# Products of zeros ahead of a decoder layer's first matrix products, two row tiles on a second load queue, and their norms in written order

## The chip, the core and the metric

The kernel runs on one core of a Trainium2 chip. The metric is device time in microseconds (us), the median of the runs. TensorE (PE) has a clock gate with two levels, 1.2 and 2.4 GHz. The other engines are VectorE (DVE), ScalarE (ACT), GpSimd (POOL) and SyncE (SP); SP issues most of the transfers, POOL the rest.

## What is computed

One step of a decoder layer, for a prompt of 2048 rows with 16 learned meta rows ahead of it, and for 64 sample rows (8 sequences of 8). The width is 1024, the type float32.

```python
hn = rmsnorm(x, g_mix_pre)                  # x * rsqrt(mean(x*x) + eps) * g
q, k, v, xl, gate = split(hn @ w_in)        # 3 * 512 + 2 * 512 columns
attn = stick_breaking_attention(q, k, v)    # the samples also read a paged cache
lru = rglru(conv4(xl)) * gelu(gate)
x = x + rmsnorm(concat(attn, lru) @ w_out, g_mix_post)
x = x + rmsnorm(relu(rmsnorm(x, g_mlp_pre) @ w_up) ** 2 @ w_down, g_mlp_post)
```

## The kernel before

The prompt is worked on in four blocks of 512 rows (`NSB = 4`). The meta rows and the samples ride along with block 0, whose input projection has 16 + 512 + 64 = 592 columns in two chunks, 0 to 272 and 272 to 592. Each float32 product is made of three TensorE products of rounded parts: `whi*ahi` (L181), `whi*alo` (L182), `wlo*ahi` (L183). Weights come in tiles of 128x1024 (`wraw`, two buffers, loaded by SP); ACT rounds one into `whi` (L158), and DVE takes the remainder into `wlo` (L159). `whi` and `wlo` have two buffers each, the products' outputs `D` four, the transposes' outputs `T` three.

What the change touches is the start, `first_norms`. It loads six row tiles: the 16 meta rows, four tiles of 128 prompt rows (x0 to x3), the 64 samples. The first weight tile's load stands behind that of x1. Each tile is squared and summed on ACT (`mean_sq`, L244), gets its `ms` on DVE (L233) and its `rstd` on POOL (L237), and is scaled in place on DVE (L397). `part(ci, k)` then transposes slice k of the three tiles of chunk ci on PE (L403) into one `T`; ACT makes `ahi` of it (L406), DVE `alo` (L407). Two parts are made at once; the other 14 are popped one by one before the products of step k in the first `gemm`: eight steps over chunk 0 (three products of 272 columns each), then eight over chunk 1 (320 columns). The last two steps have no part left to pop.

The order of PE's instructions is the written one, for the whole program: `with tc.manual_schedule(engines={ET.PE})`. The order of ACT, DVE, POOL and SP is chosen by the planner of the tile framework from its own estimates, except in the few stretches that also name them. An engine executes its instructions strictly in the order that it was given. `prep` (L420 to L429) loads and scales the rows of the next block in the buffers `y` that x0 to x3 leave; the planner has put it beside the first `gemm`.

Of the kernel before, what the change touches and what calls it, by code (L numbers as in the profile page):

```python
# [8 lines left out]
F32 = mybir.dt.float32  # L9
F32R = mybir.dt.float32r  # L10
# [3 lines left out]
ALU = mybir.AluOpType  # L14
PSUM = bass.MemoryType.PSUM

P = 128
# [16 lines left out]
ET = mybir.EngineType  # L34
# [45 lines left out]
def program(tc, I, O, NSB, NSC):  # L80
    with tc.manual_schedule(engines={ET.PE}):
        _program(tc, I, O, NSB, NSC)


def _program(tc, I, O, NSB, NSC):

    nc = tc.nc
# [4 lines left out]
    def pool(name, side="left", space=None):  # L92
        kw = {"space": space} if space else {}
        cm = tc.tile_pool(name=name, bufs=1, side=side, reuse_waits="tile", **kw)
        p = cm.__enter__()
        pools[side].append((p, cm))
        return p
# [6 lines left out]
    def T(p, shape, dt, tag, bufs=1):  # L104
        uid[0] += 1
        return p.tile(shape, dt, name=f"{tag}_{uid[0]}", tag=tag, bufs=bufs)
# [3 lines left out]
    wp = pool("wp")  # L110
# [3 lines left out]
    def psD():  # L114
        return T(ps, [P, 512], F32, "D", 4)

    def psT():
        return T(ps, [P, 512], F32, "T", 3)
# [3 lines left out]

    ident = T(const, [P, P], F32, "ident")
    nc.sync.dma_start(ident, I["ident"])


    seq = []
# [18 lines left out]
    def w_load(n):  # L146
        if n < len(seq) and n not in wraw:
            t = T(wp, [P, 1024], F32, "wraw", 2)
            nc.sync.dma_start(t, seq[n].rearrange("p a b -> p (a b)"))
            wraw[n] = t  # L150
# [79 lines left out]
    def rstd_of(parts, rows):  # L230
        ms = T(xp_, [P, 1], F32, "ms", 7)
        if len(parts) == 1:
            nc.vector.tensor_scalar(ms[:rows], parts[0], EPS, None, op0=ALU.add)  # L233
        else:
            nc.vector.scalar_tensor_tensor(ms[:rows], parts[0], EPS, parts[1], op0=ALU.add, op1=ALU.add)
        r = T(xp_, [P, 1], F32, "rstd", 7)
        nc.gpsimd.tensor_tensor(r[:rows], ms[:rows], nhalf[:rows], op=ALU.pow)  # L237
        return r

    def mean_sq(src, rows):  # L240
        junk = T(xp_, [P, DM], BF16, "junk", 1)
        ss = T(xp_, [P, 1], F32, "ss", 20)
        w = src.shape[-1]
        nc.scalar.activation(junk[:rows, 0:w], src, AF.Square, scale=1.0 / 32.0, accum_out=ss[:rows])  # L244
        return ss[:rows]

    def xsrc(s, j):
        return I["x_prompt"][(4 * s + j) * P:(4 * s + j + 1) * P, :]
# [129 lines left out]
    def first_norms(p1, ahi, alo):  # L378

        st = lambda: T(p1, [P, DM], F32, "vst", 2)  # L380
        y = lambda: T(xp_, [P, DM], F32, "y", 4)
        tiles = [(0, NMETA, I["meta_tokens"], st)]
        tiles += [(NMETA + P * j, P, xsrc(0, j), y) for j in range(4)]
        tiles.append((NMETA + SB, NSAMP, I["x_sample"], st))
        gT = T(const, [P, 2, KC], F32, "gT")
        xts = []
        for i, (col, rows, src, new) in enumerate(tiles):
            xt = new()
            nc.sync.dma_start(xt[:rows], src)
            xts.append(xt)  # L390
            if i == 2:
                w_load(0)
            if i == 0:
                nc.sync.dma_start(gT, I["gT"])
        for (col, rows, src, _), xt in zip(tiles, xts):
            r = rstd_of([mean_sq(xt[:rows, :], rows)], rows)
            nc.vector.tensor_scalar(xt[:rows], xt[:rows], r[:rows], None, op0=ALU.mult)  # L397

        def part(ci, k):
            t = psT()  # L400
            c0 = tiles[3 * ci][0]
            for (col, rows, src, _), xt in list(zip(tiles, xts))[3 * ci:3 * ci + 3]:
                nc.tensor.transpose(t[:, col - c0:col - c0 + rows], xt[:rows, k * P:(k + 1) * P], ident[:rows, :rows])  # L403
            n = col + rows - c0
            h = ahi[:, k, c0:c0 + n]
            nc.scalar.activation(h, t[:, 0:n], AF.Identity, scale=gT[:, 0, k:k + 1])  # L406
            nc.vector.scalar_tensor_tensor(alo[:, k, c0:c0 + n], t[:, 0:n], gT[:, 0, k:k + 1], h.bitcast(F32),  # L407
                                           op0=ALU.mult, op1=ALU.subtract)

        todo = [(ci, k) for ci in range(2) for k in range(KC)]  # L410
        for _ in range(2):
            part(*todo.pop(0))

        def step(ci, k):
            if todo:
                part(*todo.pop(0))

        return step, gT
# [692 lines left out]
    ahi = T(pa, [P, KC, W], F32R, "ahi")  # L1111
    alo = T(pa, [P, KC, W], F32R, "alo")
    first, gT = first_norms(p1, ahi, alo)
    K = consts(p1, gT)
    work.side = [("s", ("kv", 0), lambda: sample_attn(K, p1))]
# [178 lines left out]
```

## Time and profile before

| | |
|---|---|
| runs | 2788.22, 2781.06 and 2786.87 us; median 2786.87 |
| the profiled execution | 2790.22 us, span 2788.3 us |
| PE busy | 2688.2 us, 96% of the span |
| DVE, ACT, POOL busy | 65%, 52%, 18% |
| mean granted clock of PE | 0.985 of full speed |

The span is the time from the first to the last instruction of the profile; the 1.9 us around it are start and end. Busy shares say which engine is loaded, not which one sets the end of a stage. The matmuls' ends are modelled, so spacing from start to start is what shows PE's pace.

### The profile page before, as it was taken

How to read it: one execution, taken by the hardware profiler on the slowest of the kernel's cores; microseconds unless marked ns; L12 is line 12 of the kernel's file. 1: busy time of each engine (PE TensorE's matmuls, PEld its weight loads, DVE VectorE, ACT ScalarE, POOL GpSimd, SP SyncE). 2: the span in 40 equal slices, each digit the busy share in tenths (PEclk: the TensorE clock that was granted, in tenths of full speed). 3: DMA queues.
4: the chain of work that ended last, by engine and by line, in shares of the span. 5: the costliest groups of instructions: out<-in, count | busy, mean ns of one | idle time of the engine just before them, and what ended most of it. 6: DMA issues, size and time to landing. Idle time of an engine off the chain costs nothing.

```text
span 2788.3 us, 36998 instructions
## 1 busy us (share of the span) xinstructions
PE 2688.2 (96%) x13804; PEld 2219.4 (80%) x13804; DVE 1814.3 (65%) x2790; ACT 1451.6 (52%) x2426; POOL 515.5 (18%) x711
## 2 busy tenths in 40 slices
PE   8999988998899999999999999999999999999998
PEld 6886766777688888887788888878888887998996
DVE  5456364686777777788867777798686436433434
ACT  6556364575665655565555555665555234332332
POOL 5336361341211101112110001120000002000002
PEclk9999998999999999999999999999999999999999
DMA  4465855467534433345443333454333334322223
GB/s 161 134 208 189 261 152 171 134 169 221 166 92 128 119 115 106 106 138 154 154 110 115 103 111 103 138 162 143 105 96 104 112 119 144 99 84 77 83 84 113
DMA packets 177316, 368.23 MB, mean 132 GB/s; under 512 B 49153, under 2 KB 79361, under 8 KB 177137
## 3 DMA queue, kind: packets, MB, share of 16 engines
q1 hardware_dynamic: 103792, 287.35, 32.2%
q0 software_dynamic: 73344, 78.52, 11.3%
q8 instruction: 109, 1.79, 0.3%
q14 instruction: 71, 0.57, 0.1%
HBM read 305.51 MB, written 60.04 MB: 131 GB/s over the span
## 4 chain that ended last, share of the span: by engine, by line
PE 80%; DVE 7%; DMA 5%; POOL 3%; issue 3%; ACT 2%; SPq 0%; POOLq 0%; DVEq 0%; ACTq 0%
PE D L181 11%; PE D L183 11%; PE D L182 11%; PE D L213 10%; PE D L214 10%; PE D L215 10%; PE T L712 4%; PE T L702 4%; PE O L734 2%; PE O L736 2%; DVE wlo L159 1%; DMA md<-pb 1%; DVE pb L648 1%; POOL rstd L237 1%; DMA q<-qd 1%
## 5 line engine op out<-in xcount | busy, mean ns | idle before, releaser
L159 DVE TENSOR_TENSOR wlo<-wraw,whi 128x1024 fp32r<-128x1024 f32 x368 | 464.2, 1261 | 496.1 <-ACT whi L158 495.8
L181 PE MATMUL D<-ahi,whi 128*128 128x512 f32 (+3 forms) x1920 | 709.2, 369 | 0.0
L183 PE MATMUL D<-ahi,wlo 128*128 128x512 f32 (+3 forms) x1920 | 686.3, 357 | 2.0 <-DVE wlo L159 2.0
L182 PE MATMUL D<-alo,whi 128*128 128x512 f32 (+3 forms) x1920 | 685.0, 357 | 2.8 <-DVE alo L1017 1.5
L158 ACT CAST whi<-wraw 128x1024 fp32r<-128x1024 f32 x368 | 386.6, 1050 | 485.5 <-PE D L214 282.8
L213 PE MATMUL D<-whi,uh 128*128 128x512 f32 x1024 | 418.1, 408 | 0.0
L183 PEld LDWEIGHTS D<-ahi,wlo 128*128 128x128 f32 x1920 | 364.8, 190 | 53.2 <-DVE wlo L159 2.9
L181 PEld LDWEIGHTS D<-ahi,whi 128*128 128x128 f32 x1920 | 365.2, 190 | 51.9 <-issue 8.7
L214 PE MATMUL D<-whi,ul 128*128 128x512 f32 x1024 | 405.2, 396 | 0.0
L215 PE MATMUL D<-wlo,uh 128*128 128x512 f32 x1024 | 404.3, 395 | 0.0
L182 PEld LDWEIGHTS D<-alo,whi 128*128 128x128 f32 x1920 | 365.7, 190 | 45.5 <-DVE alo L1017 1.7
L640 ACT ACTIVATE keep<-T,nbias 128x512 f32<-128x512 f32 (+6 forms) x352 | 209.7, 596 | 241.7 <-PE T L702 234.6
L648 DVE TENSOR_TENSOR_SCAN pb<-keep,carry 128x513 f32<-128x513 f32 (+1 forms) x228 | 270.3, 1186 | 71.9 <-ACT keep L640 69.9
L724 DVE TENSOR_TENSOR wtl<-T,wth 128x512 fp32r<-128x512 f32 (+1 forms) x320 | 191.0, 603 | 73.7 <-ACT wth L723 72.6
L723 ACT CAST wth<-T 128x512 fp32r<-128x512 f32 (+1 forms) x320 | 166.1, 523 | 127.6 <-PE T L712 122.7
L215 PEld LDWEIGHTS D<-wlo,uh 128*128 128x128 f32 x1024 | 192.7, 188 | 46.7
L213 PEld LDWEIGHTS D<-whi,uh 128*128 128x128 f32 x1024 | 192.9, 188 | 39.9 <-DVE uf L1032 0.4
L214 PEld LDWEIGHTS D<-whi,ul 128*128 128x128 f32 x1024 | 193.3, 189 | 38.6
L652 DVE TENSOR_TENSOR beta<-beta,pb 128x512 f32<-128x512 f32 (+7 forms) x360 | 208.2, 578 | 0.0
L641 ACT ACTIVATE beta<-T,bias 128x512 f32<-128x512 f32 (+6 forms) x352 | 208.2, 591 | 0.0
L712 PE MATMUL T<-ident,beta 128*128 128x128 f32 (+1 forms) x1216 | 193.7, 277 | 14.1 <-ACT beta L641 7.6
L702 PE MATMUL T<-kv,q 128*128 128x512 f32 (+5 forms) x640 | 180.4, 364 | 10.3 <-ACT beta L641 4.4
(235 smaller groups left out, 3600.0 us busy)
## 6 DMA issues: line engine op xcount, KB each, us to landing
wraw<-in_w_up SPq DMA_DIRECT2D x128, 512.0 KB, 3.5
wraw<-in_w_down SPq DMA_DIRECT2D x128, 512.0 KB, 3.5
wraw<-in_w_in SPq DMA_DIRECT2D x64, 512.0 KB, 3.9
q<-qd POOLq DMA_DIRECT2D x32, 512.0 KB, 16.9
wraw<-in_w_out SPq DMA_DIRECT2D x32, 512.0 KB, 3.5
kv<-kd POOLq DMA_DIRECT2D x48, 256.0 KB, 4.1
kv<-vd POOLq DMA_DIRECT2D x48, 256.0 KB, 4.2
y<-in_x_prompt SPq DMA_DIRECT2D x16, 512.0 KB, 5.6
```

The source lines that it names most:

```text
L158: nc.scalar.copy(hi, r)
L159: nc.vector.tensor_tensor(lo, r, hi.bitcast(F32), op=ALU.subtract)
L181: nc.tensor.matmul(o, whi[:, k, :], ahi(k, a, b), start=(k == 0), stop=False)
L182: nc.tensor.matmul(o, whi[:, k, :], alo(k, a, b), start=False, stop=False)
L183: nc.tensor.matmul(o, wlo[:, k, :], ahi(k, a, b), start=False, stop=(k == KC - 1))
L213: nc.tensor.matmul(o, h, whi[:, kk, :], start=st, stop=False)
L214: nc.tensor.matmul(o, l, whi[:, kk, :], start=False, stop=False)
L215: nc.tensor.matmul(o, h, wlo[:, kk, :], start=False, stop=sp)
L640: nc.scalar.activation(keep[:, o:512], S, AF.Sigmoid, bias=nbias, scale=-0.125)
L648: nc.vector.tensor_tensor_scan(pb[:, o:513][:, ::-1], kr, kr, 1.0 if carry is None else carry, op0=ALU.mult, op1=ALU.bypass)
L702: nc.tensor.matmul(o, H["q"][:, e, i * P:(i + 1) * P], kap, start=(e == 0), stop=(e == 1))
L712: nc.tensor.transpose(t[0:kn, i * P:(i + 1) * P], w[:, c0:c0 + kn], ident)
```

## The change

A tile of zeros is made at the start, in one of the two buffers of `wlo`, by a memset of 640 columns on DVE. TensorE multiplies 128 of its columns with 512 others, 13 times, before anything else; two more such products stand between the first transposes of the meta tile and of x0, and six between those of x0 and x1. Their output, one of the four `D` buffers, is never read. The loads of x0 and x1 go through ScalarE's queue instead of SP's. The norms of the meta tile, x0 and x1 are issued in the written order on DVE, ACT and POOL, that is, tile by tile.

```diff
+    idle = T(wp, [P, 1024], F32R, "wlo", 2)
+    nc.vector.memset(idle.bitcast(F32)[:, 0:640], 0.0)
+    idle_out = psD()
+
+    def idling(n):
+        for _ in range(n):
+            nc.tensor.matmul(idle_out, idle[:, 512:640], idle[:, 0:512], start=True, stop=True)
+
+    idling(13)
...
             xt = new()
-            nc.sync.dma_start(xt[:rows], src)
+
+            (nc.scalar if i in (1, 2) else nc.sync).dma_start(xt[:rows], src)
             xts.append(xt)
...
-        for (col, rows, src, _), xt in zip(tiles, xts):
+        with tc.manual_schedule(engines={ET.DVE, ET.Activation, ET.Pool}):
+            for (col, rows, src, _), xt in list(zip(tiles, xts))[:3]:
+                r = rstd_of([mean_sq(xt[:rows, :], rows)], rows)
+                nc.vector.tensor_scalar(xt[:rows], xt[:rows], r[:rows], None, op0=ALU.mult)
+        for (col, rows, src, _), xt in list(zip(tiles, xts))[3:]:
             r = rstd_of([mean_sq(xt[:rows, :], rows)], rows)
             nc.vector.tensor_scalar(xt[:rows], xt[:rows], r[:rows], None, op0=ALU.mult)
...
-            for (col, rows, src, _), xt in list(zip(tiles, xts))[3 * ci:3 * ci + 3]:
+            for i, ((col, rows, src, _), xt) in enumerate(list(zip(tiles, xts))[3 * ci:3 * ci + 3]):
+                if (ci, k) == (0, 0):
+                    idling((0, 2, 6)[i])
                 nc.tensor.transpose(t[:, col - c0:col - c0 + rows], xt[:rows, k * P:(k + 1) * P], ident[:rows, :rows])
```

## Rows read from the trace of the kernel before

**Rows 1.** The page, part 1: busy us (share of span) xinstructions.

```profile
PE 2688.2 (96%) x13804; PEld 2219.4 (80%) x13804; DVE 1814.3 (65%) x2790; ACT 1451.6 (52%) x2426; POOL 515.5 (18%) x711
```

**Rows 2.** The chain that ended last, 0 to 36 us: start us, us, what.

```profile
2.59 4.58 DMA y<-in_x_prompt
7.25 1.16 ACT junk L244 x2
8.67 1.69 POOL rstd L237
10.38 0.76 DVE y L397
11.19 2.14 PE T L403 x7
```

**Rows 3.** Timeline of PE, 12 to 36 us: start us, us, engine, line, op.

```profile
12.98 0.57 PE L181 MATMUL D<-ahi,whi 128*128 128x272 f32 x1
...
14.49 0.57 PE L181 MATMUL D<-ahi,whi 128*128 128x272 f32 x1
...
27.88 0.47 PE L182 MATMUL D<-alo,whi 128*128 128x320 f32 x1
28.15 0.47 PE L183 MATMUL D<-ahi,wlo 128*128 128x320 f32 x1
...
29.27 0.41 PE L181 MATMUL D<-ahi,whi 128*128 128x320 f32 x1
29.52 0.30 PE L182 MATMUL D<-alo,whi 128*128 128x320 f32 x1
29.66 0.31 PE L183 MATMUL D<-ahi,wlo 128*128 128x320 f32 x1
...
30.33 0.42 PE L181 MATMUL D<-ahi,whi 128*128 128x320 f32 x1
...
35.28 0.41 PE L182 MATMUL D<-alo,whi 128*128 128x320 f32 x1 [1.33 <-DVE alo L407]
```

**Rows 4.** Windows: length, busy us by engine, PE's granted clock, DMA share, GB/s.

```profile
12.90:29.20 16.30, 16.30 (x62) 12.60 (x61) 9.58 (x36) 8.00 (x18) 7.30 (x10) 1.00 0.72 242
...
411.90:420.00 8.10, 0.47 (x9) 0.16 (x8) 3.42 (x5) 0.48 (x1) 2.54 (x6) 0.69 1.02 253
420.00:425.00 5.00, 4.94 (x24) 2.83 (x25) 0.74 (x1) 1.52 (x3) 1.41 (x4) 0.50 0.28 66
425.00:440.00 15.00, 15.00 (x71) 12.40 (x70) 7.34 (x16) 7.88 (x18) 3.92 (x7) 0.99 0.80 224
440.50:446.50 6.00, 0.10 (x1) 0.00 (x0) 3.42 (x5) 2.66 (x5) 0.00 (x0) 0.93 0.65 175
446.50:452.50 6.00, 5.89 (x17) 4.95 (x18) 2.49 (x9) 2.04 (x6) 0.00 (x0) 0.50 0.53 168
```

**Rows 5.** Window from the first `alo` to the last: PE, PEld, DVE, ACT, POOL.

```profile
12.25:35.25 23.00, 21.70 (x90) 16.56 (x88) 14.71 (x54) 12.72 (x26) 8.37 (x11) 1.00 0.66 215
```

**Rows 6.** Timeline of SP, 0 to 60 us.

```profile
2.12 0.91 SPq L389 DMA_DIRECT2D y<-in_x_prompt  x2
```

**Rows 7.** DMA view, 0 to 60 us: rate in 40 slices of 1.5 us.

```profile
GB/s 0 92 211 380 352 412 426 205 96 78 93 206 396 317 186 303 347 412 260 25 33 273 161 344 251 3 101 249 0 0 0 41 309 5 0 134 227 0 0 0
```

**Rows 8.** Timeline of ACT, 0 to 60 us.

```profile
0.74 1.28 ACT L244 ACT_TABLE_LOAD   x1 [0.74 <-PEq L1286]
3.59 1.05 ACT L244 ACTIVATE junk<-vst 16x1024 bf16<-16x1024 f32 x1 [1.56 <-DMA vst<-in_meta_tokens]
...
11.70 0.49 ACT L406 ACTIVATE ahi<-T,gT 128x272 fp32r<-128x272 f32 x1 [0.49 <-PE T L403]
12.10 1.06 ACT L244 ACTIVATE junk<-y 128x1024 bf16<-128x1024 f32 x1
...
13.16 0.47 ACT L406 ACTIVATE ahi<-T,gT 128x272 fp32r<-128x272 f32 x1
```

**Rows 9.** Timeline of POOL, 0 to 60 us.

```profile
7.34 0.56 POOL L237 TENSOR_TENSOR rstd<-ms,nhalf 128x1 f32<-128x1 f32 x1 [1.82 <-DVE ms L233]
```

## The prediction

> **What bounds the kernel now.** I read the page first: PE is busy 96% of the span [rows 1], so what shortens PE's own work, or brings its work forward, counts. The change lies in the first 36 us, so next comes the chain of waits there. It begins with the load of x1, which ends at 7.2 us, and goes through x1's square, its rstd on POOL, its scale on DVE and into the transposes at 11.19 [rows 2]. From there PE itself is the chain.
>
> PE's timeline then shows the pace [rows 3]. In chunk 0 a step (three products of 272 columns and a part's transposes) takes 14.49 - 12.98 = 1.51 us. Two products of 320 columns follow each other after 0.27 us at 27.88, and after 0.14 us at 29.52: 320 columns in 0.27 us are 1.2 GHz, in 0.14 us some 2.3. So the clock rises at about 29.2, after 16 us in which PE was never idle by its busy time (first row of [rows 4]). The granted clock in that row reads 1.00 all the same; for the start of the program I go by the spacing. Later the column does show the gate: it fell in two pauses of PE, 8.1 and 6.0 us long, then stood at 0.50 for about 5.0 and 5.9 us of dense products, and was back at 0.99 behind the first [rows 4]. So dense products raise it in 5 to 6 us, while products mixed with float32 transposes took 16. At the higher level a step with its transposes takes 30.33 - 29.27 = 1.06 us [rows 3]. The first gemm ends after a wait of 1.33 us for the last `alo`, at 35.28 [rows 3].
>
> **The fillers.** The zeros need a DVE memset of 640 columns, at most the 0.76 us that a pass over 1024 columns takes [rows 2], on a DVE that has nothing to do yet. They can be there by some 1.6 us (PE, ACT and DVE begin at about 0.8). Thirteen products of 512 columns at 1.2 GHz are 13 x 0.427 = 5.55 us: they end at 7.15 at the latest. Before, PE did its first transpose at 9.3, so this lies in idle time. The two next cost at most 0.85, behind a transpose of 0.3: 8.3. The six then end, with x0's transpose of 0.5, at 10.1 at the higher level and at 11.4 at the lower. x1's transposes stood at 11.19: without the rise the fillers eat the lead and 0.2 us more, and with it they leave 1.1 us. With the 5.0 and 5.9 us of [rows 4] the rise comes between 6.6 and 7.5, before the six, and the pauses that remain are shorter than 2 us, far from those in which the clock fell. No row shows that products of zeros count like others; that is the first rival.
>
> **The loads and the written order.** SP issued x0 and x1 from 2.12 on, at 0.46 us each [rows 6]. ACT can issue from about 0.75, and its table load of 1.28 us, shifted behind the two issues, ends near 2.9, before the meta tile's square at 3.59 [rows 8]; if the table load stays first, this saves nothing. In the first 4.5 us the rate had hardly come up, 92 and 211 GB/s, against about 390 after that [rows 7]: at most 1.5 x (390 - 92 + 390 - 211) = 0.7 MB was missed. The earlier start regains about 1.1 us of the stream for x0, but x1 now runs beside the first weight tile, which SP issues two places earlier (as it does all its later loads, 0.9 us sooner). From its landing x1 needs 1.16 (square), 0.26 (ms), rstd, 0.76 (scale). Its rstd took 1.69 us while DVE scaled two tiles; alone x0's took 0.56 [rows 2, 9]. With the tiles in order DVE has scaled the meta tile and x0 before. The new wait, the meta tile's scale for its rstd, has `ms` of x0 and all scales behind it on DVE, but x0's square ends later than that scale, so nobody is kept. That is worth up to 1.1 us even if x1 lands no earlier. Together x1's transposes can come 0.5 to 2.3 us sooner, and the fillers cap this at about 1.1. I take a lead of 1.0, between 0 and 1.1.
>
> The Trainium skill, page "DMA: Bandwidth & Descriptors", section "Issuing engines are not separate DMA queues", speaks against the second queue: transfers started by several engines interleave on the same 16 DMA engines, and only issue time is saved. By that rule x1 gains no bandwidth from ACT's queue and the lead would be nearer 0.5, the sum below 6.8; no row of before has two such queues, so the trace can't say.
>
> **The first gemm at the higher clock.** Take the stretch from the first `alo` to the end of the last: 23.0 us, in which DVE works 14.71 and ACT 12.72 [rows 5]. PE at the higher level would need eight steps of chunk 0 at 1.06 less 3 x 48 columns at 2.4 GHz (0.06), six of chunk 1 with a part at 1.06, and one without (0.45): 8.0 + 6.4 + 0.45 = 14.8 us. So PE and DVE become equally long, and the gain can't be the whole difference: DVE's queue is strict, and it waits in it for rstd and for ACT. The 1.33 us at the end are such a wait, and they stay unless the planner writes another order. The first steps don't speed up either: ACT has `ahi` at 11.70 and 13.16 with the square of x3, 1.06 us, between them [rows 8], and the samples' square behind. So 14.8 plus 1.3 is 16.1 as the lower bound, and 18.1 the upper one, at which two more steps keep their 1.5 us pace and two further waits on rstd of 0.5 come in. I take 16.7, close to the lower one because only the first three of 16 parts have a square beside them. Gain: 23.0 - 16.7 = 6.3 us, between 4.9 and 6.9.
>
> **What is late next.** Behind the first gemm stands the second. The loads that it and `prep` need run on DMA engines that are loaded to 66% in this stretch [rows 5]; those of `prep` are released by PE's own transposes, which leave the buffers `y`, so they move forward with it. `wlo`'s buffer for the zeros is free from 10 us on, before the second weight tile wants it, and the extra `D` only rotates the four. These cost nothing. All later stages start from the first gemm's results, so a lead there should come through to the end.
>
> **Sum.** 1.0 + 6.3 = 7.3 us. The profiled execution took 2790.2 us (span 2788.3 and 1.9 around it): 2782.9. It lies 3.35 us above the median of the runs shown, so the median should go from 2786.9 to 2779.6, 0.26% less. Bounds: 0 + 4.9 and 1.1 + 6.9, that is 2782.0 to 2778.9; with some 3 us for small shifts in the waits of later stages the forecast's own range is 2776 to 2784.
>
> **Rivals.** First, the clock isn't up for the first gemm: zeros don't raise it, or the rise comes late. For it speaks that 16 us of steady work did not raise it before; against it, the two dense stretches. It gives at most the lead, -0.2 to 1.1: 2786. The Trainium skill, "TensorE: Matmul & The Clock Gate", Part 1, says that the number of slow products before the rise varies between executions of one kernel; by it some runs would get this and others the forecast. [rows 4] shows 5.0 and 5.9 us, a spread of that kind.
>
> Second, DVE and ACT become the bound more thoroughly: each scale, square and `alo` waits for the other engine in turn, and half of the gain is lost, 3.5 us: 2783.5. For it speaks that DVE's 14.7 us have to go into some 16.5; against it, steps of 1.06 us were kept for three steps with both engines at work [rows 3].
>
> Third, slower: the planner orders ACT, DVE, POOL and SP anew for the whole program, and the start's shift gives a place in the attention stage one more pause of PE like those at 411.9 and 440.5 [rows 4]. One costs its 6 to 8 us and half of the 5 to 6 us at the lower clock, 9 to 11: with one the median is 2789, with two 2799. From the second on it decides. The same may take one away: 2770.
>
> Fourth, the loads are hidden anyway and the change of queue does nothing; that is in the bounds of the lead.
>
> **How the numbers follow.** Forecast 0.66; first rival 0.10; second 0.10; one or two pauses more 0.09, of which two 0.04; one pause fewer 0.05. A difference under 0.3%, 8.4 us, can't be told from none here: the runs shown spread over 7 us. The forecast's 7.3 lies just inside, and about two fifths of its range lie beyond: 0.27, and with the lost pause 0.05 that is 0.32 faster. Slower are the two pauses and a little, 0.05. The rest, 0.63, is within. The range 2773 to 2789 leaves out the two pauses, the lost pause and the forecast's far end, under 2 in 10.
>
> **What would show it.** Filler products from about 1.5 us, spaced 0.43 us and then 0.21 before the last six. The first L181 at about 12, steps of 1.0 to 1.1 us from the third on, the second gemm's first product some 7 us sooner. DVE above 85% busy between. The pauses at 411.9 and 440.5 there again, some 7 us earlier. Steps of 1.5 us behind full-pace fillers would show that the clock fell again; steps above 1.2 us at the higher clock that DVE holds PE up. Wrong would be a difference that arises behind 100 us.

## The result, and the profile after

The changed kernel takes 2793.51 us (median of 20 runs, 2787.47 to 2799.46), the one before 2786.89 (20 runs, 2781.06 to 2794.96): ratio on record 1.0021, 95% interval 1.0014 to 1.0027. By the medians it is slower by 6.6 us, where 7.3 less had been forecast. The profiled execution took 2790.52 us, near the low end of its runs, and that of before 2790.22, in the upper part of its own; so the pair of traces hides the difference at its end, and the start has to be read by itself.

The page hardly moves against [rows 1]:

```profile
PE 2690.5 (96%) x13825; PEld 2219.3 (80%) x13825; DVE 1814.5 (65%) x2791; ACT 1452.1 (52%) x2426; POOL 516.0 (19%) x711
```

The 21 more products are those of zeros. PE's timeline of the first 40 us (start, us, engine, line, op, count, and in brackets the idle time before it with what ended it) shows where they went; the first product of the first gemm is L192 at 16.68, against 12.98 in [rows 3], and the second gemm starts at 39.42, against 35.68, first here from before and then the changed kernel:

```profile
35.68 0.29 PE L181 MATMUL D<-ahi,whi 128*128 128x272 f32 x1
```

```profile
1.59 5.15 PE L133 MATMUL D<-wlo 128*128 128x512 f32 x13 [1.59 <-DVE keep L652]
11.07 0.28 PE L421 MATMUL T<-ident,vst 16*128 16x16 f32 x1 [4.32 <-DVE ms L244]
11.28 1.22 PE L133 MATMUL D<-wlo 128*128 128x512 f32 x2
...
12.69 2.91 PE L133 MATMUL D<-wlo 128*128 128x512 f32 x6
15.39 0.41 PE L421 MATMUL T<-ident,y 128*128 128x128 f32 x1
...
16.68 0.37 PE L192 MATMUL D<-ahi,whi 128*128 128x272 f32 x1
18.16 0.40 PE L193 MATMUL D<-alo,whi 128*128 128x272 f32 x1 [1.11 <-DVE alo L425]
...
20.13 0.57 PE L192 MATMUL D<-ahi,whi 128*128 128x272 f32 x1
...
21.64 0.57 PE L192 MATMUL D<-ahi,whi 128*128 128x272 f32 x1
...
32.24 0.42 PE L193 MATMUL D<-alo,whi 128*128 128x320 f32 x1 [1.35 <-DVE alo L425]
...
39.42 0.43 PE L192 MATMUL D<-ahi,whi 128*128 128x272 f32 x1
```

The 13 products end at 6.75, as forecast. Then PE is idle for 4.32 us. The windows (length, busy us of PE, PEld, DVE, ACT, POOL, granted clock, DMA share, GB/s) answer to [rows 4, 5]:

```profile
6.80:11.00 4.20, 0.00 (x0) 0.00 (x0) 2.01 (x4) 2.93 (x5) 0.54 (x1) 0.78 1.04 354
11.07:15.80 4.73, 4.68 (x12) 2.89 (x12) 3.22 (x13) 3.72 (x8) 2.79 (x5) 0.50 0.55 97
16.70:19.40 2.70, 1.59 (x11) 1.17 (x9) 2.35 (x10) 0.95 (x4) 2.22 (x4) 1.00 1.00 393
19.50:26.00 6.50, 6.50 (x27) 5.25 (x26) 3.94 (x13) 3.12 (x6) 3.42 (x4) 0.50 0.77 222
26.30:32.90 6.60, 5.25 (x30) 3.89 (x29) 4.62 (x19) 4.88 (x10) 0.58 (x1) 1.00 0.61 235
33.10:39.40 6.30, 6.30 (x22) 5.21 (x22) 2.66 (x8) 1.59 (x4) 0.58 (x2) 0.50 0.28 93
```

A granted clock of 0.50 is the lower level, 1.2 GHz, and 1.00 the higher, 2.4 GHz. So zeros do raise the clock: its first recorded rise is at 5.7 us, before the first transpose. But it falls at 9.1, in the idle time behind them, comes back at 16.0, falls behind the wait that ends at 18.16, and once more behind the one that ends at 32.24. Of the 22.7 us of the first gemm 13.2 run at 0.50, with the old 1.51 us a step (20.13 to 21.64).

Who is late? ACT's timeline, against [rows 8], where the meta tile's square started at 3.59 and the first `ahi` at 11.70:

```profile
0.74 0.90 ACTq L401 DMA_DIRECT2D y<-in_x_prompt  x2
1.67 1.28 ACT L255 ACT_TABLE_LOAD   x1 [1.67 <-PEq L1304]
5.67 1.06 ACT L255 ACTIVATE junk<-vst 16x1024 bf16<-16x1024 f32 x1 [2.72 <-DMA vst<-in_meta_tokens]
...
8.06 1.04 ACT L169 CAST whi<-wraw 128x1024 fp32r<-128x1024 f32 x1 [1.23 <-DMA wraw<-in_w_in]
9.01 1.05 ACT L255 ACTIVATE junk<-y 128x1024 bf16<-128x1024 f32 x1
...
13.73 1.06 ACT L255 ACTIVATE junk<-vst 64x1024 bf16<-64x1024 f32 x1
...
15.84 1.08 ACT L424 ACTIVATE ahi<-T,gT 128x272 fp32r<-128x272 f32 x2 [0.96 <-PE T L421]
```

and the chain of waits against [rows 2]:

```profile
2.12 5.92 DMA wraw<-in_w_in
8.06 1.05 ACT whi L169
...
10.28 0.74 DVE vst L410
```

The chain no longer begins with x1's load but with the weight tile's. The planner, which orders ACT, DVE and POOL from its own estimates, has put the cast of that tile (L169) ahead of x0's square on ACT, and `wlo` (9.13 to 10.3) ahead of the meta tile's scale on DVE; the meta tile's `rstd` had been there for 2.7 us when that scale began. SP's and POOL's timelines, against [rows 6, 9]:

```profile
2.12 0.80 SPq L160 DMA_DIRECT2D wraw<-in_w_in  x1
2.96 0.91 SPq L401 DMA_DIRECT2D y<-in_x_prompt  x2
```

```profile
7.08 0.54 POOL L248 TENSOR_TENSOR rstd<-ms,nhalf 16x1 f32<-16x1 f32 x1 [2.40 <-DVE ms L244]
```

SP issues the weight's load at 2.12, where x0's stood before. Behind the cast stand the squares of the other five tiles and, on DVE, all six scales ahead of the first `alo`:

```profile
17.62 0.90 DVE L425 SCALAR_TENSOR_TENSOR alo<-T,gT,ahi 128x272 fp32r<-128x272 f32 x2
```

And the meta tile's small load is there for its reader 2.1 us later, beside the 1.05 MB of x0 and x1 on ACT's queue, all of whose packets have moved by 6.2 us; [rows 7] becomes, in the first slices of 1.5 us,

```profile
GB/s 0 167 374 290 393 412 328 166 89 70 113 333 407 243 216 224 216 126 418 374 205 0 0 0 22 259 399 19 96 259 0 0 0 210 150 0 0 90 259 0
```

1.5 x (167 + 374 + 290 - 92 - 211 - 380) = 0.2 MB more by 6 us, of the 0.7 that were thought to be the most.

### The profile page after: what moved, and what is told of

Same layout as the page of the kernel before. It is cut to its first block, busy times and chain, and to the rows that moved or that the text cites. A ratio compares the mean times of both kernels' runs of the same rounds, so it can differ in the third digit from the quotient of the medians.

```text
span 2788.7 us, 37040 instructions
## 1 busy us (share of the span) xinstructions
PE 2690.5 (96%) x13825; PEld 2219.3 (80%) x13825; DVE 1814.5 (65%) x2791; ACT 1452.1 (52%) x2426; POOL 516.0 (19%) x711
## 3 DMA queue, kind: packets, MB, share of 16 engines
q10 hardware_dynamic: 288, 1.05, 0.1%
## 4 chain that ended last, share of the span: by engine, by line
PE 80%; DVE 7%; DMA 5%; POOL 3%; issue 2%; ACT 2%; SPq 0%; another core or an unknown queue 0%; POOLq 0%; DVEq 0%; ACTq 0%
PE D L192 11%; PE D L194 11%; PE D L193 11%; PE D L224 10%; PE D L225 10%; PE D L226 10%; PE T L730 4%; PE T L720 4%; PE O L752 2%; PE O L754 2%; DMA x1d<-y 1%; DVE wlo L170 1%; DVE pb L666 1%; POOL rstd L248 1%; DMA md<-pb 1%
## 5 line engine op out<-in xcount | busy, mean ns | idle before, releaser
L192 PE MATMUL D<-ahi,whi 128*128 128x512 f32 (+3 forms) x1920 | 707.3, 368 | 0.7 <-ACT ahi L1034 0.7
L169 ACT CAST whi<-wraw 128x1024 fp32r<-128x1024 f32 x368 | 386.6, 1050 | 491.8 <-PE D L225 284.5
L192 PEld LDWEIGHTS D<-ahi,whi 128*128 128x128 f32 x1920 | 364.2, 190 | 52.4 <-issue 8.5
```

Source lines behind the costliest of these rows:

```text
L169: nc.scalar.copy(hi, r)
L192: nc.tensor.matmul(o, whi[:, k, :], ahi(k, a, b), start=(k == 0), stop=False)
```

## The experiments

Fourteen kernels beside the two, and both of these again; a ratio is to runs of before on the same chip. First the list; "second gemm" is the start of its first product in the profiled execution, "ratio" the one on record to before in the same batch. The recorded ratio isn't exactly that of the medians: for the changed kernel those give 1.0024 in the first batch, for all in order without zeros 1.0008 instead of 1.0001.

| kernel | products of zeros | x0, x1 on | first product | second gemm | ratio, 95% |
|---|---|---|---|---|---|
| before, three profiles | - | SP | 12.8 to 13.0 | 35.7, 32.9, 31.6 | 1 |
| changed, three profiles | 21 | ACT | 16.5 to 17.5 | 39.4, 41.2, 42.1 | 1.0021, 1.0018 |
| zeros alone | 21 | SP | 16.7 | 36.0 | 1.0007 (0.9997 to 1.0018) |
| loads alone | - | ACT | 15.9 | 36.4 | 1.0019 (1.0006 to 1.0033) |
| written order alone | - | SP | 15.3 | 35.8 | 1.0013 (0.9999 to 1.0026) |
| changed without zeros | - | ACT | 16.0 | 38.9 | 1.0019 (1.0006 to 1.0032) |
| changed, cast behind x1 | 21 | ACT | 14.9 | 37.0 | 1.0008 (0.9999 to 1.0017) |
| the same | 21 | SP | 14.9 | 35.2 | 1.0010 (1.0000 to 1.0020) |
| all in order | 21 | SP | 11.6 | 33.5 | 1.0007 (0.9994 to 1.0021) |
| all in order, no zeros | - | SP | 12.7 | 30.3 | 1.0001 (0.9986 to 1.0015) |
| all in order, ACT's queue | 21 | ACT | 15.4 | 43.3 | 1.0031 (1.0019 to 1.0044) |
| norms between the steps | 21 | SP | 11.7 | 38.6 | 1.0020 (1.0009 to 1.0032) |
| the same, no zeros | - | SP | 12.2 | 36.9 | 1.0013 (1.0003 to 1.0024) |
| waits filled | 21 + 29 | SP | 11.5 | 36.1 | 1.0016 (1.0004 to 1.0028) |
| next rows behind | 21 + 12 | SP | 11.8 | 30.0 | 1.0003 (0.9993 to 1.0012) |
| the same, no zeros | - | SP | 12.0 | 30.1 | 0.9989 (0.9977 to 1.0000) |

A profile is one execution and a ratio stands for a dozen, and still the two go together: over the 16 entries with a ratio of their own (first profile for the changed kernel's first ratio, second for its second) a second gemm that starts 1 us later goes with 0.65 us more at the end (straight line through them, correlation 0.90). So most of what sets these kernels apart comes from the start, and about two thirds of it come through. The line reaches a ratio of 1 at 30.9 us, though, while the three starts of before average 33.4: a start earlier than that of before bought nothing in all in order without zeros (30.3, 1.0001).

**Parts alone.** Each takes the other two parts out of the change; for the loads alone, against before:

```diff
-            nc.sync.dma_start(xt[:rows], src)
+            (nc.scalar if i in (1, 2) else nc.sync).dma_start(xt[:rows], src)
```

Zeros alone:

> Only the 21 products of zeros are added; loads and norms as before. Theory A (the second load queue makes the planner put the first weight tile's cast, which waits for a load, ahead of x0's square): the start is not delayed here, x1's transposes stay near 11.2 to 11.5 us, the clock is up for at least part of the first gemm, and the median falls by 2 to 6 us. Theory B (the fillers themselves cost, standing between the transposes at half clock, with a clock that falls again): the first gemm ends 1 to 3 us later than before and the median rises by 2 to 5 us.

Loads alone:

> Only the loads of x0 and x1 go through ScalarE's queue; no fillers, no written order. Theory A: the meta tile lands about 2 us later (near 5.6 us), the cast of the first weight tile stands ahead of x0's square and holds it back to about 9 us, the first gemm starts 3 to 4 us later than 12.98, and the median rises by 3 to 5 us. Theory B: nothing is lost here, median within 2 us of before.

Written order alone:

> The third part of the change alone: norms of the meta tile, x0 and x1 in written order on DVE, ACT and POOL, no products of zeros, all loads on SP. If the written order frees x1's rstd from behind two scales, x1's transpose comes 0.5 to 1 us sooner than 11.19; if the planner fills the space around it with squares that wait for loads, the first ahi comes at 13 to 15 instead of 11.70, and the second gemm up to 2 us later. Median within 2 us of before either way.

The changed kernel without its products of zeros:

> The changed kernel without its products of zeros: loads on ACT's queue and written order only. If the queue move through the planner's order is the whole loss (the kernel with the moved loads alone: 1.0019): ratio 1.001 to 1.003, first ahi at 14.5 to 16.5, second gemm at 35 to 39, as in the changed kernel within 2 us. If the products of zeros cost something of their own there (x1's transpose held 1.4 us by six of them at the lower clock): 1.5 to 4 us less than the changed kernel.

The loads alone cost 5.4 us (2793.80 against 2788.39), with and without the written order, and the zeros add nothing measurable to it (1.0019 without, 1.0021 and 1.0018 with). Their ACT timeline has the order of the changed kernel, without a single product of zeros:

```profile
5.50 1.06 ACT L246 ACTIVATE junk<-vst 16x1024 bf16<-16x1024 f32 x1 [2.55 <-DMA vst<-in_meta_tokens]
...
8.01 1.04 ACT L160 CAST whi<-wraw 128x1024 fp32r<-128x1024 f32 x1 [1.36 <-DMA wraw<-in_w_in]
8.96 1.05 ACT L246 ACTIVATE junk<-y 128x1024 bf16<-128x1024 f32 x1
...
14.86 1.04 ACT L409 ACTIVATE ahi<-T,gT 128x272 fp32r<-128x272 f32 x2
```

The parts add up to more than the whole (0.0007, 0.0019 and 0.0013 against 0.0021), by an amount that intervals of 0.0010 to 0.0014 either way leave open. Each of them alone makes the planner put squares of x2, x3 or the samples ahead of the first `ahi`, which came at 16.18, 14.86 and 13.99 (11.70 in before).

**The cast.** One line at the end of the written stretch of the changed kernel, with the loads on ACT's queue and on SP's:

```diff
+            w_split(0)
```

> The changed kernel, with the first weight tile's cast and remainder named in the written order behind the three norms. Theory A: x0's square no longer waits for the weight's load; x1 is scaled near 11 us instead of 14.0, the first gemm ends 3 to 6 us sooner than in the changed kernel, and the median is 2 to 5 us below that of before. Theory B: x1's transposes still wait for the fillers, no more than 1.5 us are regained, and the median stays above before.

> As the run before, with x0 and x1 back on SP's queue: fillers, written order and the cast behind it. Theory A: the meta tile lands at 3.6 us again and x0 at 5.9; x1 is scaled near 10 us, the first gemm ends near 30 to 33 us against 35.7 before, and the median is 3 to 6 us below before, the best of these four. If the second queue itself is worth something, it is slower than the run with it. Theory B: fillers hold x1's transposes back, gain under 2 us.

With the cast behind x1's scale more than half of the loss is gone (2.6 us are left), and the queue then makes no difference that these runs could show (2790.94 and 2790.46). The first product starts at 14.9 in both, held by `ahi` (waits of 1.38 and 2.88 us ahead of it), which stands behind the squares of x2, x3 and the samples. So the cast was one item of the planner's order, not the whole.

**All in order.** The norms, the first cast and the first three parts are written out, each `ahi` and `alo` as soon as its transposes are there:

```diff
...
+        with tc.manual_schedule(engines={ET.DVE, ET.Activation, ET.Pool}):
+            for i in range(3):
+                scale(i, stats(i))
+            w_split(0)
+            r = stats(3)
+            part(*todo.pop(0))
+            scale(3, r)
+            part(*todo.pop(0))
+            r = stats(4)
+            part(*todo.pop(0))
+            scale(4, r)
+            scale(5, stats(5))
...
```

> The fillers stay; x0 and x1 go back to SP's queue; DVE, ACT and POOL get a written order in which the first ahi and alo stand as soon as their transposes are there: the squares of x3 and of the samples, which wait for loads, stand behind them. Theory C (the planner's order is what kills the start: in the changed kernel the first ahi came at 15.84 behind squares that waited for loads, 11.70 before, and PE waited 4.3 us ahead of the first transpose): the first ahi comes at about 11.5, the first real product at about 13, and with the clock up by 16 to 20 us the second gemm begins at 30 to 33 (35.7 before, 39.4 in the changed kernel); the median lies 2 to 5 us under before. Rival D (the clock falls in the sparse start whatever the order, so the fillers buy nothing): second gemm at 35 to 36.5, median within 1.5 us of before.

> The same written order and SP's queue, without any product of zeros. Theory C: the order alone puts the first product at 12.5 to 13 and the second gemm at 34 to 35.7, the median within 1.5 us of before and 2 to 4 us above the same order with fillers. Rival D: the same as the kernel with fillers within 1 us. If the clock rises by itself as early as 23.6 us, as it did in the kernel with the moved loads alone, the second gemm begins at 32 to 34 here too, and the fillers are not needed.

> The same written order with fillers, but x0 and x1 loaded through ACT's queue as in the changed kernel. If the second queue's harm went through the planner's order alone (the weight's cast ahead of x0's square), this equals the kernel with SP's queue within 1 us. If the loads themselves are the harm (the meta tile lands 2 us later because x0's 512 KB share the DMA engines with it), the meta tile's square starts at 5.5 instead of 3.6 and x1's scale 0.5 to 1.5 us later: second gemm 1 to 2 us later and the median 0.5 to 2 us above the one with SP's queue.

With SP's queue the first product starts at 11.60, and the kernel is 2.7 us above before (2787.52 against 2784.86) where the changed one, beside it, is 5.9 above (2790.78). Without zeros it starts at 12.74; with the same zeros, the same queue and only the cast written, it started at 14.89. So with SP's queue and this order the start isn't late, with zeros or without: what makes it late is the planner's order, whichever part of the change sets it off. Theory C's gain doesn't come, though: no better than before, and the zeros make no difference (2786.99 without them). ACT's queue costs 7.6 us here (2795.09), and its late start comes again through the order more than through the landing: the meta tile's square is 2.5 us later and x1's transpose 1.2 (11.65 against 10.45), but the first `ahi` 3.8, because the planner has put a small constant of another stage (L352), whose operands come through DVE from small loads that land late, ahead of it:

```profile
14.62 0.20 ACT L352 ACTIVATE spad<-spad 128x4 f32<-128x4 f32 x1 [3.31 <-DVE spad L351]
14.85 0.87 ACT L416 ACTIVATE ahi<-T,gT 128x272 fp32r<-128x272 f32 x2
```

The rest is the clock: it fell at 14.8, in PE's wait of 2.41 us for that `ahi`, and stayed down to 45.5, so the first gemm took 27.9 us (15.39 to 43.25) where it took 21.9 with SP's queue (11.60 to 33.51).

**The same kernels again.** Three profiles of each in all.

> The changed kernel once more, beside the others on one chip, for a second profile. Theory C: the same starts, first ahi at 15 to 16.5 and second gemm at 38 to 40, and a median 4 to 8 us above before, since order and landings don't vary. Rival D: the profile's late rise at 39.9 us was that execution's own, and here the clock is up by 30 us and the second gemm begins at 35 to 37.

> A third profile of the changed kernel. The first product at 16.5 to 17.6 as in the other two, at whatever moment the clock rises; the clock up by 4 to 8 us through the products of zeros, and down again before the second gemm begins, at 37 to 42.

> The kernel before, unchanged, for a second profile. If the late rise of the clock at 29.2 us belongs to the kernel, it rises at 27 to 31 us again and the second gemm begins at 35 to 36.5. If the moment of the rise varies between executions of one program (the kernel with the moved loads alone rose at 23.6, the one with all in order and without fillers at 17.7), it rises anywhere from 17 to 30, and the second gemm begins at 30 to 35.7; then the profile that the prediction was made from was one of the late ones, and the gain that the prediction put on the clock was partly there already in most runs of before.

> A third profile of the kernel before. The first product at 12.8 to 13.0 as in the other two; if the moment of the rise is a draw (29.2 and 19.3 in the two so far), it lies anywhere from 17 to 30, and the second gemm begins at 31 to 35.7. If the first was the exception: 18 to 21, and the second gemm at 32 to 33.5.

Here lies what the prediction's base was missing. Products of 272 columns in the third profile of before, around the rise:

```profile
18.93 0.57 PE L181 MATMUL D<-ahi,whi 128*128 128x272 f32 x1
...
19.50 0.29 PE L183 MATMUL D<-ahi,wlo 128*128 128x272 f32 x1
...
20.08 0.37 PE L181 MATMUL D<-ahi,whi 128*128 128x272 f32 x1
...
31.19 0.42 PE L182 MATMUL D<-alo,whi 128*128 128x320 f32 x1 [1.34 <-DVE alo L407]
...
31.60 0.30 PE L181 MATMUL D<-ahi,whi 128*128 128x272 f32 x1
```

The step that begins at 18.93 is the last slow one; from 20.08 on a product follows after 0.12 to 0.23 us. The rise comes at 19.5 here and at 19.3 in the second profile, against 29.2 in the first, with the same instructions and a first product at 12.9 in each. The three starts of the second gemm average 33.4 in before and 40.9 in the changed kernel, 7.5 us apart and without overlap; 4.0 of them are the first product's, 3.5 the longer first gemm (24.0 against 20.5 us on average). The three profiled executions of each end 3.8 us apart on average, the medians 6.6 and 5.9. The profile from which the prediction was made, with the late rise, took 2790.22 us; the two with the early rise took 2783.34 and 2785.85, so part of the 3.35 us by which the first lay above the median is that rise.

Much can still move behind the start. Matched instruction by instruction, PE in the first profile of the changed kernel is 3.4 us behind that of before from 50 to 350 us and 0.4 us behind from 1850 us on. It regains 2.1 us of that in one stage (before, then changed; granted clock 0.92 and 1.00):

```profile
1290.00:1335.00 45.00, 39.20 (x189) 31.37 (x188) 40.31 (x61) 26.04 (x48) 18.26 (x24) 0.92 0.62 197
```

```profile
1290.00:1335.00 45.00, 38.33 (x197) 30.49 (x196) 41.83 (x64) 27.73 (x52) 19.02 (x25) 1.00 0.65 202
```

Which kernel gets the fall there changes with the execution: the second and third profiles of before read 1.00 and 0.92 in this window, those of the changed kernel 0.89 and 1.00.

**Between the steps.** The norms of x2, x3 and the samples moved into steps 0 to 3 of chunk 0 (`stats` at step k, `scale` at step k + 1), and the second weight's cast to step 2 of chunk 1.

> Fillers and SP's queue, as in the kernel with all in order, and the squares and scales of x2, x3 and the samples moved between the steps of chunk 0, so that the alo that PE waited 1.45 us for at 16.9 us has no 64-row scale ahead of it. Theory C: no wait of over 0.5 us ahead of the last steps of chunk 1, no fall of the clock there, and the second gemm at 28 to 30 us; median 0 to 5 us below the kernel with all in order. Rival E (what the first gemm gains it meets again in the squares of the next block's rows, which stand in ACT's order ahead of the last ahi and wait for loads that PE's own transposes release): a wait of 1 to 3 us for ahi in chunk 1 at 24 to 29 us whatever the start, second gemm at 30 to 33.

> The same without products of zeros. If fillers are worth something once the order leaves PE no waits: the second gemm 2 to 5 us later than with them, and the median 1 to 4 us above. If the clock rises by itself at about 18 us in this order, as in the other kernel without fillers: the same within 1.5 us.

A miss: PE waited for an `alo` behind a scale (1.43 us at 18.07) and for the samples' scale (1.77 us at 23.42). The clock, up from 7.5, fell at 17.8 and stayed down to 38.3.

**Waits filled.** Products that nobody reads, on operands that are there, where the kernel with all in order had waited (5 more ahead of step 4 of chunk 1, 12 more in it):

```diff
...
+                if first and (ci, k) in ((0, 3), (1, 4)):
+                    for _ in range(12):
+                        nc.tensor.matmul(idle_out[:, 0:272], whi[:, 0, :], ahi(0, 0, 272), start=True, stop=True)
...
```

> The kernel with all in order and fillers, and more products that nobody reads (272 columns, operands that are already there, to the same unused output) in the places where PE waited: 12 after the first product of step 3 of chunk 0 (wait of 1.45 us there), 5 ahead of step 4 of chunk 1 and 12 after its first product (0.62 and 1.34 us). Theory F (the waits in the sparse gemm are what makes the clock fall): the clock, once up at 5 to 7 us, stays up until the second gemm, which begins at 29.5 to 31.5 (33.5 without these products); median 1 to 4 us below the 2787.5 of the kernel without them, as ratios to before. Rival G (it falls in the mix of transposes and products whatever fills the waits): it falls again between 12 and 25 us, the second gemm at 32 to 36.

Without them PE waited 1.45 us at 16.92, and the clock fell at 17.4. With them:

```profile
15.24 1.67 PE L199 MATMUL D<-ahi,whi 128*128 128x272 f32 x12
...
27.04 0.41 PE L196 MATMUL D<-ahi,whi 128*128 128x320 f32 x1 [1.56 <-ACT ahi L423]
28.79 0.41 PE L200 MATMUL D<-alo,whi 128*128 128x320 f32 x1 [1.34 <-DVE alo L424]
```

```profile
5.40:29.10 23.70, 18.76 (x103) 13.55 (x103) 16.27 (x55) 15.59 (x30) 10.71 (x13) 1.00 0.86 294
29.30:32.50 3.20, 3.20 (x15) 2.75 (x14) 2.24 (x9) 1.13 (x4) 0.76 (x2) 0.50 0.02 6
```

The clock stays up for 24 us and falls behind the next two waits. Theory F holds as far as these places show it: in this run the mix of transposes and products, with its waits filled, did not bring the clock down. The number missed: the waits of chunk 1 had moved one step ahead, so the 17 products there filled nothing and were pure cost, over 3 us, most of it at the lower clock. What PE waits for at 27 us is told by ACT and SP. The next block's rows are loaded (L461) into the buffers that x0 and x1 leave, so the load begins with PE's last transpose of them; their square stands on ACT ahead of the last `ahi`:

```profile
18.80 0.80 SPq L461 DMA_DIRECT2D y<-in_x_prompt  x2
```

```profile
25.42 1.06 ACT L262 ACTIVATE junk<-y 128x1024 bf16<-128x1024 f32 x1 [2.93 <-DMA y<-in_x_prompt]
```

A faster chunk 0 releases the load sooner, but it takes 6.5 us and its square and scale come behind it, and chunk 1 at the higher clock needs no more than 8: part of the time gained is waited for there. In the changed kernel's second profile that wait was 3.03 us.

**The next rows behind.** Two transposes more of x0 and x1 in the last part, to columns that nobody reads, so that their buffers come free only there and the planner puts those squares behind the last `ahi`; the 12 products of step 3 of chunk 0 stay, the 17 of chunk 1 are out:

```diff
+            if (ci, k) == (1, 7):
+                for xt in xts[1:3]:
+                    nc.tensor.transpose(t[:, 384:512], xt[:, 0:P], ident)
```

> All in order with fillers, 12 products that nobody reads in the wait of 1.45 us of step 3 of chunk 0, and two transposes of x0 and x1 more at the end of the last part (to columns that nobody reads), so that the buffers of x0 and x1 come free only there: the loads of the next block's rows, and with them their squares on ACT, stand behind the last ahi. Theory F with rival E (the waits make the clock fall, and the last waits are those for the next block's rows): the clock, up at 5 to 7.5 us, stays up, no wait over 0.5 us in chunk 1, the second gemm at 29 to 30.5; median 2 to 5 us below before if a lead at the start comes through to the end, within 1.5 us of before if later stages swallow it.

> The same order and the same late release of x0's and x1's buffers, without any product that nobody reads. The clock rises where the draw puts it, 17 to 30 us, and doesn't fall again before the second gemm, which begins at 30 to 34.5; median 1 to 3 us above the one with fillers. If the products of zeros are worth nothing even here: equal within 1 us.

The wait for the next rows is gone, and with products of zeros the clock is up throughout, from 6.4:

```profile
6.50:30.00 23.50, 21.57 (x122) 15.95 (x121) 17.36 (x60) 15.27 (x30) 9.76 (x13) 1.00 0.76 247
```

And yet the second gemm starts no sooner than without them, 29.99 against 30.12, where the clock had risen by itself at 19.8. The windows of the eight steps of chunk 0, first with zeros, then without:

```profile
11.80:22.01 10.21, 9.98 (x62) 7.67 (x61) 8.62 (x32) 7.03 (x15) 6.49 (x9) 1.00 0.71 210
```

```profile
12.02:22.69 10.67, 10.67 (x50) 8.53 (x49) 7.50 (x28) 6.29 (x15) 6.87 (x8) 1.00 0.71 218
```

(In the second the clock column reads 1.00 from the start of the program, while the steps are 1.51 us long to 19.62.) With the higher clock in all of it instead of its last 3 us, chunk 0 is only 0.46 us shorter. DVE works 8.62 of 10.21 us, and 12 of PE's products were there only to fill a wait. The lead of 0.68 us at the end of chunk 0 (22.01 against 22.69) is gone one step later, where PE waits for an `alo`:

```profile
22.78 0.42 PE L196 MATMUL D<-alo,whi 128*128 128x320 f32 x1 [0.36 <-DVE alo L423]
```

In the kernel with zeros the second weight's `wlo` (20.97, 1.23 us of DVE) stands ahead of that `alo`; without zeros it comes later. So the two kernels differ in the planner's order too, and what a higher clock would be worth in one and the same order isn't shown.

The kernel without zeros is the fastest of all, 2782.01 against 2785.80 of before in its batch, 0.9989 with an interval that touches 1. The one with zeros is slower by 5.3 us in the medians and by 3.6 in the means. Its trace stays within 0.2 us of the other from 36 to 200 us and ends 3.7 behind. The largest step between them is in the stage named above, with zeros and without:

```profile
1290.00:1335.00 45.00, 37.50 (x172) 29.79 (x171) 38.13 (x55) 25.13 (x45) 17.63 (x22) 0.89 0.54 167
```

```profile
1290.00:1335.00 45.00, 38.55 (x199) 30.93 (x197) 40.93 (x60) 26.65 (x49) 17.34 (x22) 1.00 0.61 195
```

From 1280 to 1360 us a lead of 1.4 us turns into a lag of 3.0. So in this pair of traces the difference arises behind the start; whether the dozen runs of each differ for the same reason stays open.

## Why the prediction was wrong

**The lead (forecast +1.0 us, measured at the first product -3.5 to -4.7 between three profiles of each kernel).** This step failed first. Each duration in it held: issues on ACT from 0.74, the table load behind them done at 2.95, and x0 and x1 moved by 6.2 us, where x1 had landed at 7.2 [rows 2]. What failed is that they were laid along the order of before. That "nobody is kept" was said of the meta tile's scale; but that scale stood behind `wlo`, that behind the cast, and that waited for the weight's load until 8.06. The weight's load is issued two places earlier, and the planner's new order put its cast first. The loads alone and the changed kernel without zeros show the same, and the kernel with all in order and SP's queue has its first product 5 us sooner. On ACT's queue x0 was issued 1.4 us sooner, and x1 was there about 1.0 us sooner, while the meta tile's square moved from 3.59 to 5.67. The Trainium skill, "DMA: Bandwidth & Descriptors", section "Issuing engines are not separate DMA queues", says that transfers started by several engines interleave on the same DMA engines and that only the time to issue them is saved. The traces agree. What decided was neither: x1, there sooner, was squared later (10.18 against 7.25), behind the cast.

**The pauses "shorter than 2 us".** The longest was 4.32 us, as a consequence: the products of zeros ended at 6.75 as forecast, but the first transpose, which the working had before 8, came at 11.07. The six between x0 and x1 then ran at the lower clock, 2.91 us, and held x1's transpose from 13.98, when its scale ended, to 15.39.

**The first gemm (forecast 23.0 us down to 16.7).** In the pair of traces of the forecast it takes 22.7 us in both kernels, from its first product to that of the second gemm: the gain of 6.3 us is nothing. That zeros raise the clock was right (4.4 to 7.5 us, forecast 6.6 to 7.5). Three things were wrong. Its base was one execution: the moment of the rise is a draw, that is, it changes from execution to execution. It came at 29.2 after 16 us of steps, and at 19.3 and 19.5 after 6.4 and 6.6 us of the same steps in the others, so 2.8 to 4.1 of the 6.3 us were there already in two of the three profiles of before. The Trainium skill, "TensorE: Matmul & The Clock Gate", Part 1, says that the number of slow products before the rise varies between executions; the three profiles of before agree with it. The prediction used that rule for the changed kernel's gain and not for its own base. Second, the clock, once up, didn't stay up: it fell in all nine profiles of kernels with zeros whose waits weren't filled, and stayed up to 29 us or longer in the two with step 3 filled. Third, the limit of 16.1 us counted DVE's and ACT's work but not the loads that PE's transposes release; with those waits out and the clock up, the gemm took 18.2 us (11.80 to 29.99), of which 1.5 are the filled wait. The second rival, in which DVE and ACT hold half of the gain back, was nearest in mechanism and still too kind: with zeros or without, the gemm ends at 30.0 and 30.1.

**What is late next.** Of the next block's loads it was said that "they move forward with it": they do, but the square that waits for them stands ahead of PE's own last inputs. It was priced at nothing; it took up to 3.03 us.

**Sum and rivals.** The forecast's 7.3 us was 1.0 + 6.3; measured it is -4.0 and -3.5 at the second gemm on the mean of three profiles each, and -6.6 at the end. The first rival (the clock isn't up for the first gemm) had the right mechanism for its term, but kept the forecast's lead of -0.2 to 1.1. The third, a pause more behind 100 us, falls: from 45 us on the orders of ACT, DVE and POOL are those of before, and the longest waits of PE there are 8.2 and 6.1 us, against 7.7 and 6.0. The fourth, that the loads are hidden anyway, falls too: alone they cost 5.4 us. That the difference stays under 0.3% was given 0.63, and it does, by luck: it was reasoned for small gains, and what came is a loss. 2793.5 lies above the range up to 2789, because no case in it had a start more than 0.2 us later.

## What to carry to other kernels

Before a load or an issue is moved, ask what else the scheduler will order anew for it: here two moved loads turned the order of the first 45 us, and no duration in the trace of before could show the price; write out the order of what the engine must feed first, and then measure. Before a warm-up is priced, take several profiles of the kernel as it is, since the moment of the rise is a draw, and ask whether the stage behind it can use the clock: here chunk 0 took 10.21 us with the higher clock throughout and 10.67 with it in the last 3 us, since at the higher clock DVE (8.62 us of work) left PE waits to fill. A faster stage meets the next wait that was hidden behind its slowness, so name the transfer that it releases and what stands behind that transfer.

## What the runs showed of the hardware

- Thirteen products of zeros raise the granted clock: its first recorded rise was at 4.4 to 7.5 us in the profiles with them (first product at 1.6), and at 17.7 to 36.7 in those without.
- A wait of PE of 0.8 to 1.5 us in a sparse stage was followed by a fall in some executions (0.82 us ending at 29.06 in the second profile of before, then 0.50 to 32.9) and not in others (1.34 us ending at 31.19 in the third).
- Once down in such a stage it can stay down long: from 18.6 to 42.5 us in the third profile of the changed kernel, though PE was never idle from 18.7 to 31.0.
- At the start of the program the granted clock reads 1.00 until its first recorded change, while the spacing shows the lower level: 320 columns every 0.27 us up to 29.2 us in the first profile of before.
- A 64 KB load issued at 1.20 us on SP's queue was there for its reader at 3.3 to 3.6 us alone, and at 5.3 to 5.8 us with two 512 KB loads issued on ACT's queue from 0.75 on.
